# Opening of a hybrid attention and DeltaNet layer: vector products and column forms dealt among single rows of the early projections, and the token RMS factor as a diagonal in the transposing product

## The chip, the cores and the metric

The kernel runs on one core of a Trainium2 chip. The metric is the device time of one execution in microseconds (us), the median of several runs. All matrix products are in fp32, or as three products of split fp32r halves (high by high, high by low, low by high).

## The reference, cut to what matters

One layer over 512 latent tokens (x) and 256 context tokens (ctx), width 1024. The opening computes the modulated input of all projections:

```python
mod_lat = jax.nn.silu(c) @ w_mod + b_mod
mod_ctx = jax.nn.silu(c_ctx) @ w_mod + b_mod
sh1, sc1, g1, sh2, sc2, g2 = [m[:, None, :] for m in jnp.split(mod_lat, 6, axis=-1)]
csh1, csc1, cg1, csh2, csc2, cg2 = jnp.split(mod_ctx, 6, axis=-1)
hx = modulate(rms_norm(x), sh1, sc1)        # rms_norm(x) * (1 + sc1) + sh1, per token row
hc = modulate(rms_norm(ctx), csh1, csc1)
ak_x, av_x, qkv_x, db_x, da_x, aq_x, z_x, gate_x = split_cols(hx @ w_in)
```

Behind it come grouped-query attention, a bidirectional gated DeltaNet, their merge, and a gated MLP with a short convolution. The change touches none of these.

## The kernel before

All of it is one function, with a scheduler that fixes the order on each engine (TensorE = PE, VectorE = DVE, ScalarE = ACT, GpSimd = POOL, and SyncE = SP, which issues the loads) when the program is built. The opening is the block around `ORD`: a string of steps that sets the order of PE's products there; the other engines' work is placed by the scheduler around it. `k` counts the eight blocks of 128 channels, `kp` and `nb` four pairs of them. The steps:

- `dN`: `warm(N)`, 4N products of zeros into an unused PSUM buffer.
- `xj`, j = 0 to 11: `x_cols`. For tokens of tile i = j // 4 (ctx, first half of x, second half of x; each 2 x 128 tokens) and channel pair kp = j % 4, four 128x128 blocks are transposed into one PSUM buffer `pt`, which ACT or DVE copies to the stash (`hcL` for ctx, `hxL` for x). `pt` has two buffers. `j % 2 or j < XV` decides for ACT.
- `aN`, `bN`: `gemv`, the first and second half of the product of silu(c), silu(c_ctx) with columns of `w_mod` (tiles `wm`, 1 MB each) into `pm`; behind bN, ACT copies it to `mrow`.
- `mN`: `mod_cols`, which turns this row into per-channel columns `mod` and `modc` by small products into `xb` ("column form").
- `yN`: `modulate`, for channel pair N: `hf` = stash * scale + shift (DVE for x, ACT for ctx), split into a high part (`hxH`, `hcH`, on ACT) and a low part (`hxL`, `hcL`, on DVE).
- `pK`: `early_proj`, block K of the first two heads' key projections: for each head three products into `pc` (ctx, 256 wide) and three into `mb` (x, 512 wide). `qK` does the first head alone, `rK` the second.

Before the transposes each token tile is squared and summed (one half on ACT, one on DVE), POOL raises the mean to the power -1/2 into `rs`, and DVE multiplies the tile in place with it. `split(hi, lo, src)` and `load_w` produce `whi` on ACT and `wlo` on DVE from a loaded weight tile `wraw` (two buffers). The first two `wraw` are the weights of the early projections, the next three those of the next stage (`in_w_aq` twice, `in_w_av`). `LORD` sets the order of the first loads; x tiles and the `w_mod` tiles share eight buffers, so the last three of `w_mod` wait for the transposes of a token tile each. The next stage begins with the products `pq`.

Records in the profile: in the order below an fp32 product and a transpose are one row each.

Of the kernel before, what the change touches and what calls it, by code (L numbers as in the profile page):

```python
# [6 lines left out]
F32 = mybir.dt.float32  # L7
F32R = mybir.dt.float32r
AF = mybir.ActivationFunctionType
ALU = mybir.AluOpType  # L10
# [4 lines left out]
P = 128  # L15
D = 1024
KT = 8
# [17 lines left out]
POOLW = 0  # L35
ND, D0U = 4, 6
KV = 10
ORD = 'd4 x0 x1 x2 x3 x4 x5 x6 x7 a0 x8 x9 x10 x11 b0 d1 m0 y0 a1 p0 b1 p1 m1 y1 a2 b2 p2 m2 y2 p3 a3 b3 p4 m3 y3 p5 p6 p7'
RK = 1.0
HB = 2  # L40
WS = [1.0, 1.0, 1.0]
WY = [2.0, 2.4, 0.8, 0.8, 1.0, 2.4]
TG = 1
PMB = 1
XV, YV = 4, 0
NS = 2
MPA, MPD = .25, .14
DA = '203242'
# [21 lines left out]
C_ID, C_ONE, C_MS, C_MI, C_TRI = 0, 128, 256, 512, 768  # L70
# [5 lines left out]
def hybrid_layer_body(tc, x, ctxt, xT, consts, cols, rows, w_mod1, w_mod2, w_av, w_aq, w_cm, w_pa, w_pd, w_out,  # L76
                      w_up, w_down, outT, dbg=None):
    nc = tc.nc
    V, A, G, SP = nc.vector, nc.scalar, nc.gpsimd, nc.sync
    pinned = [False]  # L80

    class Ordered:
# [4 lines left out]
        def transpose(self, *a, **k):  # L87
            i = nc.tensor.transpose(*a, **k)
            return tc.keep_in_program_order(i) if pinned[0] else i
# [24 lines left out]
    def tt(out, a, b, op, eng=None):  # L114
        put((eng or V).tensor_tensor(out=out, in0=a, in1=b, op=op))  # L115

    def ts(out, a, s1, op0, s2=None, op1=None, eng=None):
        if op1 is None:
            (eng or V).tensor_scalar(out=out, in0=a, scalar1=s1, scalar2=None, op0=op0)
        else:  # L120
            (eng or V).tensor_scalar(out=out, in0=a, scalar1=s1, scalar2=s2, op0=op0, op1=op1)  # L121
# [4 lines left out]
    def act(out, a, f=AF.Copy, **kw):  # L126
        put(A.activation(out, a, f, **kw))  # L127
# [5 lines left out]
    def mm3(ps, wh, wl, xh, xl, k, n):  # L133
        T.matmul(ps, wh, xh, start=(k == 0), stop=False)
        T.matmul(ps, wh, xl, start=False, stop=False)
        T.matmul(ps, wl, xh, start=False, stop=(k == n - 1))

    def mm(ps, a, b, start=True, stop=True):
        T.matmul(ps, a, b, start=start, stop=stop)

    with es:
# [20 lines left out]
        cst = cr.tile([P, C_TRI], F32, name="cst")  # L162
        with sooner():
            SP.dma_start(cst[:, 0:C_MS], consts[:, 0:C_MS])
        ident = cst[:, C_ID:C_ID + 128]
# [19 lines left out]
        def rsqrt(out, a, s, eps):  # L185
            n = a.shape[1]
            ts(out, a, s, ALU.mult, eps, ALU.add)
            tt(out, out, mhalf[:, 0:n], ALU.pow, G)
# [8 lines left out]
        def mbank():  # L197
            return mmp.tile([P, 512], F32, name="mb", tag="mm")
# [50 lines left out]
        hxH = hxp.tile([P, KT, NL], F32R, name="hxH")  # L249
        hxL = Pairs()  # L250
# [190 lines left out]
        with m1_es:  # L441
            m1 = m1_es.enter_context(tc.tile_pool(name="m1", bufs=1))
            mps = m1_es.enter_context(tc.tile_pool(name="mps", bufs=NB, space=PSUM))
            xs = []
            wms = []

            def ordered_load(out, in_):
                i = SP.dma_start(out, in_)
                if LPIN:
                    tc.keep_in_program_order(i)  # L450

            hw = []
            for op in LORD.split():
                i = int(op[1])
# [11 lines left out]
                if op[0] == "h":  # L466
                    with first():
                        hi, lo = (m1.tile([P, 1024], F32R, name=n, tag=n, bufs=NS) for n in ("whi", "wlo"))
                        split(hi, lo, raw)
                        hw.append((hi, lo))  # L470
            with sooner():
                ordered_load(tabs.rearrange("p a b -> p (a b)"), consts[:, C_COS:C_END])
                ordered_load(wrow, rows[0:512].partition_broadcast(P))
            SP.dma_start(cst[:, C_MS:C_TRI], consts[:, C_MS:C_TRI])
            cs = m1.tile([P, 16], F32, name="cs")
            act(cs, col[:, S_C:S_C + 16], AF.Tanh, scale=0.5)
            stt(cs, cs, 1.0, col[:, S_C:S_C + 16], ALU.add, ALU.mult)
# [4 lines left out]
            V.tensor_reduce(out=sel, in_=ident.rearrange("p (b c) -> p c b", c=32)[:, 0:2, :], axis=AX.X, op=ALU.add)  # L482
            ss = m1.tile([P, 6], F32, name="ss")
            rs = m1.tile([P, 6], F32, name="rs")
            for i in range(3):
                junk = [hxH[:, k:k + 2, :].rearrange("p a b -> p (a b)") for k in (6, 2)]
                act(junk[0], xs[i][:, 0, :], AF.Square, accum_out=ss[:, 2 * i:2 * i + 1])
                V.scalar_tensor_tensor(out=junk[1], in0=xs[i][:, 1, :], scalar=1.0, in1=xs[i][:, 1, :], op0=ALU.mult, op1=ALU.mult,
                                       accum_out=ss[:, 2 * i + 1:2 * i + 2])
                sl = slice(2 * i, 2 * i + 2)  # L490
                rsqrt(rs[:, sl], ss[:, sl], 1.0 / D, EPS)
                for t in range(2):
                    ts(xs[i][:, t, :], xs[i][:, t, :], rs[:, 2 * i + t:2 * i + t + 1], ALU.mult)
            m2 = lambda t, o: t[:, o:o + 16].rearrange("p (s k) -> p s k", s=2)
            wsl = lambda k: slice(k * P, k * P + P)

# [24 lines left out]
            def x_cols(j):  # L521
                i, kp = j // 4, j % 4
                dst = stash[1][kp] if i == 0 else stash[0][kp][:, :, 256 * i - 256:256 * i]
                pt = mps.tile([P, 2, 256], F32, name="pt", tag="pt", bufs=NB - PMB - NS)
                for a in range(2):
                    for t in range(2):
                        transpose(pt[:, a, t * P:(t + 1) * P], xs[i][:, t, wsl(2 * kp + a)])
                if j % 2 or j < XV:
                    act(dst, pt)
                else:  # L530
                    V.tensor_copy(dst, pt)
# [18 lines left out]
            hps = []  # L550

            def early_proj(k, heads=slice(0, NS)):
                if not hps:
                    for _ in range(NS):
                        hps.append((mbank(), mps.tile([P, NCX], F32, name="pc", tag="pc", bufs=NS)))
                for (ps, pc), (hi, lo) in list(zip(hps, hw))[heads]:
                    mm3(pc, hi[:, wsl(k)], lo[:, wsl(k)], hcH[:, k, :], hcL[:, k, :], k, KT)
                    mm3(ps, hi[:, wsl(k)], lo[:, wsl(k)], hxH[:, k, :], hxL[:, k, :], k, KT)

            pinned[0] = True  # L560
            mrows, mpm = {}, {}
# [9 lines left out]
            def step(what, i):  # L571
                if what == "g":
                    with sooner():
                        gemv(i)
                elif what in "ab":
                    with sooner():
                        gemv(i, 0 if what == "a" else 4, 4 if what == "a" else KT)
                elif what == "m":
                    with sooner():
                        mod_cols(i, mrows[i])  # L580
                elif what == "d":
                    with sooner():
                        warm(i)
                elif what == "x":
                    with sooner():
                        x_cols(i)
                elif what == "y":
                    with first():
                        modulate(i)
                elif what in "qr":  # L590
                    early_proj(i, slice(0, 1) if what == "q" else slice(1, NS))
                else:
                    early_proj(i)

            for op in ORD.split():
                step(op[0], int(op[1:]))
# [81 lines left out]
        with kv_es:  # L678
# [31 lines left out]
            for blk in range(6):  # L710
# [5 lines left out]
                for t in range(6 if blk < 2 else 4):  # L716
# [4 lines left out]
                    for k in range(KT):  # L721
                        hi, lo = w2[k // wk]
                        wsl = slice((k % wk) * wn, (k % wk) * wn + wn)
# [692 lines left out]
        x1 = [x1p.tile([P, NL], F32, name=f"x1_{c}") for c in range(KT)]  # L1416
# [258 lines left out]
```

## Time and profile before

| | us |
|---|---|
| median of 3 runs | 1241.82 |
| lowest and highest run | 1236.42, 1242.31 |
| the profiled execution | 1239.93 |
| its span, first to last instruction | 1238.2 |
| PE busy | 1183.2 (96%) |
| DVE, ACT, POOL busy | 818.8, 601.7, 248.3 |
| first product of the stage behind the opening starts at | 56.28 |

Times in the rows are counted from the start of the span. A row of the timeline has the start, the time, the engine, the line, the operation, the tiles written and read, the shapes, the count, and in brackets the idle time ahead of it with what ended it. The granted clock is a share of TensorE's full clock.

### The profile page before, as it was taken

The page shows a single profiled execution, that of the slowest core. Times are in us where ns is not written, and L with a number is a line of the kernel's source. Part 1 is how long each engine was busy: PE and PEld are TensorE (multiplying, and loading weights), DVE is VectorE, ACT ScalarE, POOL GpSimd, SP SyncE. Part 2 cuts the span into 40 slices and gives each one's busy share as a digit, 9 for nine tenths or more (in the row PEclk, how much of TensorE's full clock was granted, in tenths as well). Part 3 has the DMA queues.
Part 4 walks back from the last instruction along what each step waited for, and adds up shares of the span by engine and source line. Part 5 has one row for each costly group of instructions (what it writes and reads, how often), then busy time and mean ns, then how long its engine had stood idle before and what let it go on. Part 6 is the DMA issues. An engine that isn't in the chain of part 4 may idle for free.

```text
span 1238.2 us, 20489 instructions
## 1 busy us (share of the span) xinstructions
PE 1183.2 (96%) x7753; PEld 1015.6 (82%) x7753; DVE 818.8 (66%) x1611; ACT 601.7 (49%) x1386; POOL 248.3 (20%) x334
## 2 busy tenths in 40 slices
PE   7999899999899898999999989999999999999996
PEld 5799888989787787788887678789888888888886
DVE  5648678888698657766657677866776765553333
ACT  4524477877565845744535432333544444432321
POOL 0111110100314695595574000000000000000000
PEclk8999999999999998999999999999999999999998
DMA  9413313332536426335336776862333422333331
GB/s 385 143 60 117 99 56 97 113 100 89 191 130 213 132 90 205 116 122 194 129 97 202 243 251 204 304 223 103 119 122 133 136 93 95 102 92 97 94 94 68
DMA packets 67554, 174.97 MB, mean 141 GB/s; under 512 B 7456, under 2 KB 18176, under 8 KB 66048
## 3 DMA queue, kind: packets, MB, share of 16 engines
q1 hardware_dynamic: 67456, 173.67, 41.8%
q8 instruction: 61, 1.00, 0.3%
q14 instruction: 37, 0.30, 0.1%
HBM read 146.85 MB, written 26.79 MB: 140 GB/s over the span
## 4 chain that ended last, share of the span: by engine, by line
PE 53%; DMA 4%; DVE 4%; ACT 2%; issue 1%; POOL 1%; SPq 0%; POOLq 0%; DVEq 0%; ACTq 0%
PE mc L84 33%; PE mb L84 13%; PE pb L84 5%; DMA gt<-atd 1%; DVE wlo L115 1%; DMA M<-gamdr 1%; PE pk L84 1%; ACT whi L127 0%; DMA wl<-in_w_mod_dram 0%; PE pqk L84 0%; DMA sz<-gdr 0%; POOL NN L115 0%; DMA cw<-in_rows_dram 0%; DMA Gb<-gamdr 0%; DMA NN<-gamdr 0%
## 5 line engine op out<-in xcount | busy, mean ns | idle before, releaser
L115 DVE TENSOR_TENSOR wlo<-wraw,whi 128x1024 fp32r<-128x1024 f32 (+1 forms) x153 | 188.7, 1235 | 159.9 <-ACT whi L127 159.5
L127 ACT ACTIVATE whi<-wraw 128x1024 fp32r<-128x1024 f32 (+1 forms) x153 | 159.5, 1044 | 213.8 <-PE mc L84 114.0
L84 PE MATMUL mc<-h,whi 128*128 128x512 f32 (+1 forms) x752 | 219.6, 376 | 0.3 <-ACT whi L127 0.3
L84 PE MATMUL mb<-hxH,whi 128*128 128x512 f32 x384 | 162.5, 423 | 1.6 <-DVE t L124 1.6
L84 PEld LDWEIGHTS mc<-h,whi 128*128 128x128 f32 x752 | 138.0, 188 | 26.1 <-ACT whi L127 0.5
L84 PE MATMUL mb<-hxL,whi 128*128 128x512 f32 x384 | 152.2, 396 | 0.2 <-DVE hxL L115 0.2
L84 PE MATMUL mb<-hxH,wlo 128*128 128x512 f32 x384 | 152.2, 396 | 0.0
L84 PE MATMUL mc<-h,wlo 128*128 128x512 f32 (+1 forms) x376 | 141.3, 376 | 0.5 <-DVE wlo L115 0.5
L84 PE MATMUL mc<-a,whi 128*128 128x512 f32 (+1 forms) x396 | 111.1, 366 | 0.6 <-DVE x L124 0.6
L115 POOL TENSOR_TENSOR rc<-rc,mhalf 128x2 f32<-128x2 f32 x4 | 3.0, 740 | 456.8 <-DVE rc L121 456.8
L84 PEld LDWEIGHTS mb<-hxH,wlo 128*128 128x128 f32 x384 | 73.0, 190 | 16.8
L84 PEld LDWEIGHTS mb<-hxH,whi 128*128 128x128 f32 x384 | 73.4, 191 | 11.9 <-issue 2.0
L84 PEld LDWEIGHTS mc<-a,whi 128*128 128x128 f32 x396 | 71.5, 189 | 12.9 <-DVE x L124 0.8
L84 PEld LDWEIGHTS mc<-h,wlo 128*128 128x128 f32 x376 | 70.8, 188 | 13.6 <-DVE wlo L115 1.0
L84 PEld LDWEIGHTS mb<-hxL,whi 128*128 128x128 f32 x384 | 73.5, 191 | 9.7 <-DVE hxL L115 0.5
L84 PE MATMUL mc<-a,wlo 128*128 128x512 f32 (+1 forms) x198 | 72.3, 365 | 0.0
L124 DVE SCALAR_TENSOR_TENSOR u<-mc,col,u 128x511 f32<-128x511 f32 x88 | 65.3, 746 | 1.4
L115 POOL TENSOR_TENSOR prod<-X,R 128x31 f32<-128x31 f32 (+15 forms) x93 | 55.5, 597 | 19.1 <-DVE X L115 12.3
L115 POOL TENSOR_TENSOR R<-R,prod 128x31 f32<-128x31 f32 (+15 forms) x93 | 56.5, 607 | 6.8
L84 PE MATMUL pq<-whi,hxH 128*128 128x256 f32 (+1 forms) x192 | 55.5, 289 | 0.0
L84 PE MATMUL pq<-wlo,hxH 128*128 128x256 f32 (+1 forms) x192 | 54.3, 283 | 0.1
L84 PE MATMUL pq<-whi,hxL 128*128 128x256 f32 (+1 forms) x192 | 54.2, 282 | 0.0
(323 smaller groups left out, 2692.1 us busy)
## 6 DMA issues: line engine op xcount, KB each, us to landing
wraw<-in_w_cm_dram SPq DMA_DIRECT2D x48, 512.0 KB, 3.6
wraw<-in_w_up_dram SPq DMA_DIRECT2D x44, 512.0 KB, 3.3
wl<-in_w_mod_dram SPq DMA_DIRECT2D x24, 512.0 KB, 4.9
wm<-in_w_mod_dram SPq DMA_DIRECT2D x8, 1024.0 KB, 16.6
wraw<-in_w_down_dram SPq DMA_DIRECT2D x16, 512.0 KB, 3.5
wraw<-in_w_aq_dram SPq DMA_DIRECT2D x10, 512.0 KB, 3.8
M<-gamdr SPq DMA_DIRECT2D x64, 64.0 KB, 4.5
wraw<-in_w_pa_dram SPq DMA_DIRECT2D x8, 512.0 KB, 4.4
```

Of the source, the lines that this page charges most:

```text
L84: i = nc.tensor.matmul(*a, **k)
L115: put((eng or V).tensor_tensor(out=out, in0=a, in1=b, op=op))
L124: V.scalar_tensor_tensor(out=out, in0=a, scalar=s, in1=b, op0=op0, op1=op1)
L127: put(A.activation(out, a, f, **kw))
```

## The change

Six things, all in the opening:

- `ORD` has seven warming steps ahead of the transposes and none behind; b0 runs ahead of the last two transposing steps; and most steps p become a q and an r, between which vector products and column forms stand.
- The token tiles are not scaled. Instead a diagonal matrix `dgx` with the RMS factors (identity times `rs`, 128x128 per 128 tokens) is the moving operand of the transposing product, which is an fp32 product now and no transpose.
- `XV` is 0: DVE copies out every even `pt` from the first on.
- Each step's products for x (`mb`) run ahead of those for ctx (`pc`), and a p does both heads' `mb` first.
- The load of the masks (`cst`, 256 KB) keeps its place behind the row vectors in SP's order.
- The scheduler, for this order, puts the splits of the next stage's weights elsewhere (below).

```diff
-ORD = 'd4 x0 x1 x2 x3 x4 x5 x6 x7 a0 x8 x9 x10 x11 b0 d1 m0 y0 a1 p0 b1 p1 m1 y1 a2 b2 p2 m2 y2 p3 a3 b3 p4 m3 y3 p5 p6 p7'
+ORD = 'd7 x0 x1 x2 x3 x4 x5 x6 x7 a0 x8 x9 b0 x10 x11 m0 y0 a1 q0 b1 r0 q1 m1 y1 r1 a2 p2 b2 q3 m2 y2 r3 a3 p4 b3 q5 m3 y3 r5 p6 p7'
-XV, YV = 4, 0
+XV, YV = 0, 0
...
-            SP.dma_start(cst[:, C_MS:C_TRI], consts[:, C_MS:C_TRI])
+                ordered_load(cst[:, C_MS:C_TRI], consts[:, C_MS:C_TRI])
...
+            dgs = []
...
                 rsqrt(rs[:, sl], ss[:, sl], 1.0 / D, EPS)
+                dgs.append(m1.tile([P, 2, P], F32, name="dgx", tag="dgx", bufs=3))
                 for t in range(2):
-                    ts(xs[i][:, t, :], xs[i][:, t, :], rs[:, 2 * i + t:2 * i + t + 1], ALU.mult)
+                    ts(dgs[i][:, t, :], ident, rs[:, 2 * i + t:2 * i + t + 1], ALU.mult)
...
-                        transpose(pt[:, a, t * P:(t + 1) * P], xs[i][:, t, wsl(2 * kp + a)])
+                        mm(pt[:, a, t * P:(t + 1) * P], xs[i][:, t, wsl(2 * kp + a)], dgs[i][:, t, :])
...
-                for (ps, pc), (hi, lo) in list(zip(hps, hw))[heads]:
+                some = list(zip(hps, hw))[heads]
+                for (ps, pc), (hi, lo) in some:
+                    mm3(ps, hi[:, wsl(k)], lo[:, wsl(k)], hxH[:, k, :], hxL[:, k, :], k, KT)
+                for (ps, pc), (hi, lo) in some:
                     mm3(pc, hi[:, wsl(k)], lo[:, wsl(k)], hcH[:, k, :], hcL[:, k, :], k, KT)
-                    mm3(ps, hi[:, wsl(k)], lo[:, wsl(k)], hxH[:, k, :], hxL[:, k, :], k, KT)
```

First place: DVE, from the squares of the ctx tile (the row that writes `ss`) to the first copies out of `pt`. Before:

```order
7 L488 SCALAR_TENSOR_TENSOR hxH,ss<-xs 128x1024
8 L121 TENSOR_SCALAR rs<-ss 128x2
9 L119 TENSOR_SCALAR xs<-xs,rs 128x1024 x2
10 L488 SCALAR_TENSOR_TENSOR hxH,ss<-xs 128x1024
11 L121 TENSOR_SCALAR rs<-ss 128x2
12 L119 TENSOR_SCALAR xs<-xs,rs 128x1024 x2
13 L488 SCALAR_TENSOR_TENSOR hxH,ss<-xs 128x1024
14 L531 COPY hxL<-pt 128x2x256
15 L121 TENSOR_SCALAR rs<-ss 128x2
```

And after the change, the same stretch of DVE:

```order
7 L489 SCALAR_TENSOR_TENSOR hxH,ss<-xs 128x1024
8 L121 TENSOR_SCALAR rs<-ss 128x2
9 L119 TENSOR_SCALAR dgx<-cst,rs 128x128 x2
10 L489 SCALAR_TENSOR_TENSOR hxH,ss<-xs 128x1024
11 L121 TENSOR_SCALAR rs<-ss 128x2
12 L119 TENSOR_SCALAR dgx<-cst,rs 128x128 x2
13 L489 SCALAR_TENSOR_TENSOR hxH,ss<-xs 128x1024
14 L533 COPY hcL<-pt 128x512
15 L121 TENSOR_SCALAR rs<-ss 128x2
```

Row 14 was the copy of step x4 (to `hxL`), since ACT copied x0 to x3; now it is the copy of x0 (to `hcL`), behind the squares of all three token tiles.

Second place: DVE around the third `modulate`, y2. Before, from the column form m2 on:

```order
34 L115 TENSOR_TENSOR mod<-xb,col 128x2x2
35 L115 TENSOR_TENSOR modc<-xb,col 128x2x2
36 L121 TENSOR_SCALAR hf<-hxL,mod 128x512 x2
37 L115 TENSOR_TENSOR hxL<-hf,hxH 128x512
38 L115 TENSOR_TENSOR hcL<-hf,hcH 128x256
39 L115 TENSOR_TENSOR hxL<-hf,hxH 128x512
40 L115 TENSOR_TENSOR hcL<-hf,hcH 128x256
41 L115 TENSOR_TENSOR wlo<-wraw,whi 128x1024
42 L115 TENSOR_TENSOR mod<-xb,col 128x2x2
```

After, DVE again, from m2 to m3:

```order
37 L115 TENSOR_TENSOR mod<-xb,col 128x2x2
38 L115 TENSOR_TENSOR modc<-xb,col 128x2x2
39 L121 TENSOR_SCALAR hf<-hxL,mod 128x512 x2
40 L115 TENSOR_TENSOR wlo<-wraw,whi 128x1024
41 L115 TENSOR_TENSOR hxL<-hf,hxH 128x512 x2
42 L115 TENSOR_TENSOR wlo<-wraw,whi 128x1024
43 L115 TENSOR_TENSOR hcL<-hf,hcH 128x256 x2
44 L115 TENSOR_TENSOR wlo<-wraw,whi 128x864
45 L115 TENSOR_TENSOR mod<-xb,col 128x2x2
```

The low parts of the three weight tiles of the next stage stood behind y2 (the first), between m3 and y3 (the second) and behind y3 (the third); now all three stand inside y2. ACT's high parts `whi` moved with them, and the third (the tile of `in_w_av`) now stands ahead of `mrow` of the last vector product:

```order
24 L127 ACTIVATE whi<-wraw 128x1024
25 L127 ACTIVATE hf<-hcL,modc 128x256 x2
26 L127 ACTIVATE hxH<-hf 128x512 x2
27 L127 ACTIVATE whi<-wraw 128x1024
28 L127 ACTIVATE hcH<-hf 128x256 x2
29 L127 ACTIVATE whi<-wraw 128x864
30 L127 ACTIVATE mrow<-pm 128x512
```

These are ACT's rows after the change; before, two of these `whi` stood behind that `mrow`, and the third behind the last `hxH` of the opening.

## The prediction

> **What bounds the kernel now.** I read the page first (busy times), then the clock and the busy time by stretch, then the instructions of the first 57 us in order of time, engine by engine.
>
> ```profile
> span 1238.2 us, 20489 instructions
> PE 1183.2 (96%) x7753; PEld 1015.6 (82%) x7753; DVE 818.8 (66%) x1611; ACT 601.7 (49%) x1386; POOL 248.3 (20%) x334
> 56.28:1238.20 1181.92, 1135.58 (x7494) 983.11 (x7492) 787.52 (x1546) 573.27 (x1335) 244.48 (x322) 0.99 0.41 134
> ```
>
> The third line is a stretch: length, busy time of PE, PEld, DVE, ACT and POOL (with instruction counts), granted clock, DMA share, GB/s. TensorE carries the program. Behind 56.28 us it is busy 1135.6 of 1181.9 us at a clock of 0.99, and PE's order there is the same in both kernels. So the change is worth what it moves the first product of the next stage, which starts here:
>
> ```profile
> 56.28 0.28 PE L84 MATMUL pq<-whi,hcH 128*128 128x256 f32 x1
> 23.65 1.05 PE L84 MATMUL xb<-sel,mrow 128*128 128x2 f32 x8
> 54.17 0.28 PE L84 MATMUL pc<-hcH,whi 128*128 128x256 f32 x1
> 43.88 1.92 PE L84 MATMUL pm<-wm,cs 128*32 128x512 f32 x16
> 45.74 0.39 PE L84 MATMUL pc<-hcH,whi 128*128 128x256 f32 x1
> ```
>
> The last three give prices: a step p (one k, two heads) is 56.28 - 54.17 = 2.11 us, so a single head's q or r is 1.06; a vector product in two halves (a and b) is 45.74 - 43.88 = 1.86, so a half is 0.93. The second line is m0, the first column form: I cut the opening there, into 23.65 us before it and 32.63 us behind it.
>
> Now the clock. The following stretches have the same columns:
>
> ```profile
> 7.81:11.22 3.41, 1.08 (x8) 0.89 (x8) 2.49 (x6) 1.33 (x4) 0.70 (x1) 1.00 1.01 428
> 11.22:14.64 3.42, 3.06 (x15) 2.25 (x12) 2.50 (x6) 2.71 (x6) 0.70 (x1) 0.51 1.03 434
> 14.64:18.05 3.41, 3.40 (x18) 2.35 (x20) 2.26 (x6) 1.00 (x3) 0.70 (x1) 0.50 0.99 406
> 18.05:21.46 3.41, 3.06 (x25) 1.77 (x20) 2.02 (x4) 1.86 (x3) 0.00 (x0) 0.99 1.02 423
> 24.88:28.29 3.41, 1.70 (x12) 0.69 (x5) 2.64 (x8) 2.75 (x6) 0.00 (x0) 1.00 1.03 418
> 28.29:31.71 3.42, 3.42 (x14) 2.19 (x16) 0.39 (x2) 0.00 (x0) 0.00 (x0) 0.51 1.01 417
> ```
>
> A stretch of 3.41 us in which PE is busy for 1.08 or 1.70 us is followed by one or two at half clock. The DMA runs at 406 to 434 GB/s, full, in all of them.
>
> **The first part, to m0.** The diagonals replace six scalings of 1024 columns by six of 128, and the transposes become products.
>
> ```profile
> 1.49 5.33 PE L84 MATMUL pt<-hxH 128*128 128x512 f32 x16 [1.49 <-DVE hxH L563]
> 8.99 1.42 DVE L119 TENSOR_SCALAR xs<-xs,rs 128x1024 f32<-128x1024 f32 x2 [0.82 <-POOL rs L115]
> 10.33 1.22 DVE L488 SCALAR_TENSOR_TENSOR hxH<-xs 128x1024 fp32r<-128x1024 f32 x1
> 12.64 1.42 DVE L119 TENSOR_SCALAR xs<-xs,rs 128x1024 f32<-128x1024 f32 x2 [0.82 <-POOL rs L115]
> 13.97 1.22 DVE L488 SCALAR_TENSOR_TENSOR hxH<-xs 128x1024 fp32r<-128x1024 f32 x1
> 15.12 0.69 DVE L531 COPY hxL<-pt 128x512 f32<-128x512 f32 x1
> 1230.09 0.48 DVE L119 TENSOR_SCALAR dg<-cst,rc 128x128 f32<-128x128 f32 x2 [0.88 <-POOL rc L115]
> 9.80 0.33 PE L88 MATMUL pt<-cst,xs 128*128 128x128 f32 x1 [2.98 <-DVE xs L119]
> 11.70 6.24 PE L88 MATMUL pt<-cst,xs 128*128 128x128 f32 x24 [0.22 <-ACT hcL L127]
> 11.05 1.09 ACT L127 ACTIVATE hcL<-pt 128x512 f32<-128x512 f32 x2 [0.69 <-PE pt L88]
> 20.43 1.09 PE L88 MATMUL pt<-cst,xs 128*128 128x128 f32 x8 [0.35 <-DVE hxL L531]
> L84 PE MATMUL mc<-dg,cst 128*128 128x128 f32 x16 | 3.0, 319 | 1.5 <-DVE dg L119 1.5
> L119 DVE TENSOR_SCALAR dg<-cst,rc x8: 278/284/288, 856.3 to 1230.3; 128x128 f32<-128x128 f32 x8
> 449.86 1.06 PE L84 MATMUL pb<-S,kT 128*128 128x128 f32 x8
> ```
>
> DVE: two diagonals cost 0.48 us (the dg row, the same operation at the program's end) in place of 1.42, so 0.94 is saved per token tile, 2.8 in all, on an engine with room. PE: each dg tile is used by one product, and eight of them left 16 records, so an fp32 product is two passes. A transpose left one (48 transposes in this kernel, 48 records). Eight passes of 128 columns take 1.06 us (the row at 449.86), of which some 0.17 is the drain of the last: 0.89 back to back. So an x step (four products) costs 0.89 at full clock; two steps of transposes took 1.09 at 20.43, about 0.5 each. That is 12 x 0.4 = 4.7 us more for PE. The twelve added warming products fill the idle 2.98 us ahead of 9.80 (16 took 5.33, the later ones at 0.235, so 28 end at about 9.5): free, since x0 is held by the first diagonal until 9.8 anyhow.
>
> Step x2 is where the time goes. It needs the PSUM buffer of x0 (two buffers), which ScalarE emptied at 11.05, so x2 ran at 11.70. Now VectorE empties x0 (XV = 0), and on its queue that copy stands behind the squares of x1 and x2. From the rows: first diagonals at 8.99, squares of x1 at 8.99 + 0.40 = 9.39; from squares to the next scaling 12.64 - 10.33 = 2.31, so second diagonals at 11.70, squares of x2 at 12.10; to the copy 15.12 - 13.97 = 1.15, so it starts at 13.25 and ends 0.69 later. x2 starts at 14.0 and not 11.7.
>
> From there PE has ten x steps (8.9), a0 and b0 (1.9) to m0; with two buffers a pair of steps takes 0.89 and 0.17 of drain, 0.69 of copy and 0.14 of signals, 1.89 or 0.945 a step, 0.5 more. That is 14.0 + 8.9 + 1.9 + 0.5 = 25.3 at full clock. But PE idles from about 11.5 to 14.0, more than the 2.3 us that it idled in the stretch 7.81 to 11.22, which cost it the clock. If the clock is half for one stretch of 3.4 us, 1.7 us of work are lost, of which 0.4 are waits on copies anyhow: 26.6. I take this: **m0 is 3.0 us later** (bounds: +1.7 at full clock, +4.7 with two stretches, as before had from 11.22).
>
> [...] In 11.22:14.64 PE was busy 3.06 of 3.42 us with transposes, and the clock stayed at half for another stretch. [...]
>
> **The second part, m0 to the end.** Products are the same in number: 16 x 1.06, six halves of 0.93, four column forms. Only the waits differ. They come from what modulate needs after a column form:
>
> ```profile
> 26.06 0.62 ACT L127 ACTIVATE hxH<-hf 128x512 fp32r<-128x512 f32 x1
> 26.71 0.69 DVE L115 TENSOR_TENSOR hxL<-hf,hxH 128x512 fp32r<-128x512 f32 x1 [0.77 <-ACT hxH L127]
> 27.32 0.42 DVE L115 TENSOR_TENSOR hcL<-hf,hcH 128x256 fp32r<-128x256 f32 x1
> 24.63 1.06 PE L84 MATMUL pm<-wm,cs 128*32 128x512 f32 x8
> 27.04 0.38 PE L84 MATMUL pc<-hcH,whi 128*128 128x256 f32 x1 [1.34 <-ACT hcH L127]
> L84 PE MATMUL pc<-hcH,whi 128*128 128x256 f32 x16 | 5.2, 324 | 1.8 <-ACT hcH L127 1.8
> L84 PE MATMUL pc<-hcL,whi 128*128 128x256 f32 x16 | 4.9, 308 | 1.1 <-DVE hcL L115 1.1
> L84 PE MATMUL mb<-hxL,whi 128*128 128x512 f32 x16 | 6.9, 431 | 0.2 <-DVE hxL L115 0.2
> 49.09 1.22 DVE L115 TENSOR_TENSOR wlo<-wraw,whi 128x1024 fp32r<-128x1024 f32 x1
> wraw<-in_w_av_dram SPq DMA_DIRECT2D x2, 432.0 KB, 3.5
> ```
>
> Before, the rows of the early projections list 1.8 + 1.1 + 0.2 = 3.1 us of idle PE in six waits; each also hides a drain of some 0.16 that counts as busy, so 4.05 in all. What will they be after? The column form ended at 24.63; hxH was there 2.1 us later, hxL 2.8, the first hcL 3.1. So after each m the first row waits 2.1 us less what PE has in between, and its second product another 0.45 (0.69 less 0.235).
> - y0: cover is a1, 0.93: waits 1.2 + 0.45 = 1.65.
> - y1: cover r1 and a2, 1.99: 0.1 + 0.45 = 0.55.
> - y2: cover r3 and a3, but the splits of two weight tiles (wlo, 1.22 each) now stand on VectorE between hf and hxL and between hxL and hcL. hxL comes at 3.15, hcL at 5.2: p4 takes 3.7 and not 2.1, with the 0.1 a wait of 1.7. Before, p3, a3 and b3 covered all of y2.
> - y3: cover r5 alone, 1.06: 1.05 + 0.45 = 1.5. Before, all of p5 (2.11) was cover.
>
> After 5.4, before 4.05: **1.35 us more**. The half clock at 28.29:31.71 cost 1.7; the stretch around y0 keeps its gap of 1.2 us in my sum, so I leave that cost where it is (bounds: 1.7 less, or 1.7 more with a second one).
>
> The mask load that moves behind the row vectors lets the last three loads of w_mod land up to 0.6 us earlier (256 of 1024 KB, which take 2.5). Nothing waits for that: the last of them was issued at 19.1 and landed 16.9 us later, and b3 runs behind 43.88:
>
> ```profile
> L448 SPq DMA_DIRECT2D wm<-in_w_mod_dram x1: 328/328/328, 19.1 to 19.1; - x1
> DMA to landing us min/median/max: 16.9/16.9/16.9
> ```
>
> On SP's queue the masks now stand ahead of two weight loads, but behind the same bytes in all, so those land when they did; if the masks were late themselves, nothing of the opening would see it. The cost is nothing. The four warming products d1 (0.9 us) go, too; they lay in PE's wait for mrow0, which x10 and x11 now fill, since b0 runs ahead of them.
>
> **Sum:** 3.0 + 1.35 = 4.35 us, so the opening ends at about 60.6 and the profiled execution of 1239.93 us (span 1238.2) becomes 1244.3. I take **1244**. That execution lies 1.9 us under the median 1241.82 of the three runs, which spread from 1236.42 to 1242.31; so about 0.5% (6.2 us) is what a measurement of this kernel can tell from no change.
>
> **Rivals.**
> 1. *The clock stays up.* The x steps are real products, the warming reaches to x0, and the dealt rows leave no stretch as empty as 24.88:28.29. Then m0 comes at 25.3 (+1.65), the waits cost 1.35, and the 1.7 of 28.29:31.71 goes: +1.3, 1241.2. With y2's splits hidden as well, -0.4: 1239.5. For it: the stretch 14.64:18.05, which ended at full clock. Against it: the gap of 2.5 us ahead of x2. 0.33.
> 2. *Slower beyond 0.5%: a load in ScalarE's way.* The split of the third weight tile now stands on ScalarE ahead of mrow3 and all of y3. Its load can be issued only when the first wlo has freed a buffer, 2.5 us after m2. With the 3.5 us of the row above it lands 6.4 after m2, b3 ends at 6.6, and the 0.7 that mrow3 then waits lies under q5. From a landing of some 4.9 us on PE waits, and at 6.8 the sum passes 6.2: the time is 1246.5 at that point and 1249 at 9.5 us. For it: landings of 16.9 us while the DMA was full. Against it: it is not full behind 40 us. 0.12.
> 3. *Faster beyond 0.5%.* Would need the opening to end before 50.1. PE's work from m0 on is 25.8 us, and m0 can't come before 24.8, so 50.6 is its floor without any wait. 0.05, mostly for the spread of the runs.
>
> The forecast, +2 to +6, has 0.50. Slower by over 0.5% gets 0.15 (the second rival and the forecast's upper end), faster 0.05, within 0.80. The range goes from 1237.5 (the first rival at its best, with 2 us of spread) to 1249.
>
> **What would show it.** Right: VectorE's first copy out of pt starts at about 13.3 and x2 at 14.0; x steps at 0.9 us with 96 records of pt<-dgx,xs; m0 between 25 and 27; p4 stalled for its hcL; the first pq at 60 to 61. Wrong: a clock of 1.0 through 11 to 32 us (rival 1), ScalarE waiting for the DMA of in_w_av ahead of mrow (rival 2), or a first pq before 56.

## The result: 3.8 us slower, in the size forecast

The changed kernel takes 1243.14 us (median of 20 runs), the kernel before 1239.36 (median of 20, the three shown above among them). The ratio is 1.0030, with a 95% interval of 1.0018 to 1.0043. One of the changed kernel's 20 runs took 1965.29 us at a granted clock of 0.555 and is left out of the ratio; without it the median is 1242.92. The prediction was 1244.0, from a sum of 4.35 us. The two profiled executions differ by 4.04 us: 1243.97 against 1239.93.

The page of the profile after, span and busy times:

```profile
span 1242.2 us, 20603 instructions
PE 1191.4 (96%) x7809; PEld 1025.7 (83%) x7809; DVE 817.5 (66%) x1613; ACT 600.6 (48%) x1384; POOL 247.0 (20%) x334
```

The stretch behind the opening (columns as before: length; busy time of PE, PEld, DVE, ACT, POOL; granted clock, DMA share, GB/s):

```profile
59.70:1242.20 1182.50, 1138.11 (x7495) 986.31 (x7493) 788.17 (x1548) 573.24 (x1336) 244.06 (x322) 0.99 0.41 134
```

Behind the first `pq` lie 1182.50 us, before 1181.92. So the loss is in the opening, whose end moved from 56.28 to 59.70 (3.42 us). PE's instructions there in order of time, of the changed kernel:

```profile
10.30 1.95 PE L84 MATMUL pt<-dgx,xs 128*128 128x128 f32 x16
13.22 2.05 PE L84 MATMUL pt<-dgx,xs 128*128 128x128 f32 x16 [0.97 <-ACT hcL L127]
15.81 3.99 PE L84 MATMUL pt<-dgx,xs 128*128 128x128 f32 x32 [0.54 <-DVE hcL L533]
19.73 1.06 PE L84 MATMUL pm<-wm,cs 128*32 128x512 f32 x8
...
25.59 0.95 PE L84 MATMUL xb<-sel,mrow 128*128 128x2 f32 x8
...
28.52 0.50 PE L84 MATMUL mb<-hxH,whi 128*128 128x512 f32 x1 [0.97 <-ACT hxH L127]
...
44.41 0.51 PE L84 MATMUL mb<-hxH,whi 128*128 128x512 f32 x1
45.36 0.50 PE L84 MATMUL mb<-hxL,whi 128*128 128x512 f32 x1 [0.44 <-DVE hxL L115]
47.43 0.39 PE L84 MATMUL pc<-hcL,whi 128*128 128x256 f32 x1 [0.53 <-DVE hcL L115]
48.22 1.06 PE L84 MATMUL pm<-wm,cs 128*32 128x512 f32 x8
53.35 0.49 PE L84 MATMUL mb<-hxH,whi 128*128 128x512 f32 x1 [0.87 <-ACT hxH L127]
57.53 0.46 PE L84 MATMUL mb<-hxH,whi 128*128 128x512 f32 x1
59.70 0.28 PE L84 MATMUL pq<-whi,hcH 128*128 128x256 f32 x1
```

m0, the first column form, starts at 25.59, 1.94 later than before; from m0 to `pq` it is 34.11 us, 1.48 more. DVE and ACT at the two places that the prediction speaks of, step x2 and y2:

```profile
12.59 0.58 ACT L127 ACTIVATE hcL<-pt 128x512 f32<-128x512 f32 x1
13.10 0.69 DVE L533 COPY hcL<-pt 128x512 f32<-128x512 f32 x1
44.62 1.28 DVE L115 TENSOR_TENSOR hxL<-hf,hxH 128x512 fp32r<-128x512 f32 x2
45.83 1.22 DVE L115 TENSOR_TENSOR wlo<-wraw,whi 128x1024 fp32r<-128x1024 f32 x1
46.96 0.75 DVE L115 TENSOR_TENSOR hcL<-hf,hcH 128x256 fp32r<-128x256 f32 x2
48.09 0.92 ACT L127 ACTIVATE whi<-wraw 128x864 fp32r<-128x864 f32 x1 [1.70 <-DMA wraw<-in_w_av_dram]
49.36 0.60 ACT L127 ACTIVATE mrow<-pm 128x512 f32<-128x512 f32 x1 [0.34 <-PE pm L84]
```

And the stretches of the changed kernel; the clock is the third number from the end:

```profile
11.22:14.64 3.42, 2.45 (x22) 2.26 (x21) 2.30 (x6) 1.63 (x3) 1.00 (x2) 1.00 1.02 431
14.64:18.05 3.41, 2.87 (x24) 2.60 (x23) 1.77 (x4) 0.75 (x2) 0.00 (x0) 1.00 1.00 408
24.88:28.29 3.41, 2.66 (x24) 1.74 (x23) 1.89 (x5) 2.04 (x4) 0.00 (x0) 1.00 1.00 418
28.29:31.71 3.42, 2.97 (x16) 1.55 (x17) 1.97 (x4) 1.63 (x5) 0.00 (x0) 1.00 1.02 426
52.18:55.60 3.42, 2.32 (x8) 1.52 (x7) 2.35 (x5) 2.25 (x6) 0.00 (x0) 0.80 0.04 14
55.60:59.02 3.42, 3.42 (x15) 2.96 (x15) 0.00 (x0) 0.53 (x1) 0.00 (x0) 0.70 0.00 0
```

The clock is full where before it was half (0.51, 0.50 and 0.51 in 11.22 to 18.05 and 28.29 to 31.71). Instead, p6 behind the wait for y3 runs at half clock: it takes 57.53 - 53.35 = 4.18 us, where 2.11 and the small wait in it make 2.5.

### The profile page after: what moved, and what is told of

Same layout as the page of the kernel before. It is cut to its first block, busy times and chain, and to the rows that moved or that the text cites. A ratio compares the mean times of both kernels' runs of the same rounds, so it can differ in the third digit from the quotient of the medians.

```text
span 1242.2 us, 20603 instructions
## 1 busy us (share of the span) xinstructions
PE 1191.4 (96%) x7809; PEld 1025.7 (83%) x7809; DVE 817.5 (66%) x1613; ACT 600.6 (48%) x1384; POOL 247.0 (20%) x334
## 4 chain that ended last, share of the span: by engine, by line
PE 54%; DVE 4%; DMA 3%; ACT 2%; issue 1%; SPq 0%; POOLq 0%; DVEq 0%; ACTq 0%
PE mc L84 33%; PE mb L84 14%; PE pb L84 6%; DMA gt<-atd 1%; DVE wlo L115 1%; PE pk L84 1%; DMA sz<-gdr 0%; DMA wl<-in_w_mod_dram 0%; ACT whi L127 0%; PE pqk L84 0%; DMA M<-gamdr 0%; DVE wl L394 0%; DMA tdr<-go 0%; DVE o_nt L1017 0%; ACT NN L127 0%
## 5 line engine op out<-in xcount | busy, mean ns | idle before, releaser
L124 DVE SCALAR_TENSOR_TENSOR t<-mb,col,t 128x511 f32<-128x511 f32 (+1 forms) x76 | 48.9, 644 | 10.7 <-ACT t L127 10.5
```

The lines of the kernel that those rows point to most:

```text
L124: V.scalar_tensor_tensor(out=out, in0=a, scalar=s, in1=b, op0=op0, op1=op1)
```

## The experiments

All ratios are to the kernel before, with a 95% interval. "The opening's end" is the start of the first `pq` in the one profiled execution of each. Of e5, e6 and e8 the numbers stand in the text alone. The moved load of the masks, the fifth item of the change, was not run by itself.

### e1: the dealt order alone

The kernel before, with the new `ORD` and nothing else of the change.

```diff
-ORD = 'd4 x0 ... x9 x10 x11 b0 d1 m0 y0 a1 p0 b1 p1 m1 y1 a2 b2 p2 m2 y2 p3 a3 b3 p4 m3 y3 p5 p6 p7'
+ORD = 'd7 x0 ... x9 b0 x10 x11 m0 y0 a1 q0 b1 r0 q1 m1 y1 r1 a2 p2 b2 q3 m2 y2 r3 a3 p4 b3 q5 m3 y3 r5 p6 p7'
```

> The kernel before with the changed ORD alone (seven warming steps, b0 ahead of x10, dealt q and r); transposes, scaled token tiles, XV = 4 and the old order of mb and pc stay. My theory (the products in fp32 make m0 late, the dealt order costs some 1.5 us behind m0): m0 comes at about 21.5 us, since the transposes run at full clock behind the warming and x8 is held by the scaling of the last token tile; behind m0 34 us as in the changed kernel; first pq at 55.5 to 56, so 0 to 1 us faster than before. Rival (the dealt order is what costs, whatever the transposes do): first pq at 58 or later, 2 us or more slower. Rival (the dealt order gains, and the products eat it): first pq at 53 to 54, 2 to 3 us faster.

Measured: 1245.35 us, ratio 1.0052 (1.0032 to 1.0071). PE's rows in order of time, and then two stretches of this kernel:

```profile
21.55 1.05 PE L84 MATMUL xb<-sel,mrow 128*128 128x2 f32 x8
26.22 0.58 PE L84 MATMUL pc<-hcH,whi 128*128 128x256 f32 x1 [2.62 <-ACT hcH L127]
61.57 0.28 PE L84 MATMUL pq<-whi,hcH 128*128 128x256 f32 x1
```

```profile
24.88:28.29 3.41, 1.90 (x5) 1.51 (x6) 2.21 (x5) 2.11 (x5) 0.00 (x0) 0.53 1.01 416
28.29:31.71 3.42, 3.42 (x14) 1.10 (x14) 0.00 (x0) 0.60 (x1) 0.00 (x0) 0.50 1.02 424
```

m0 came 2.1 us earlier than before, and the opening ended 5.3 later. With little work left between m0 and y0's first row PE waits 2.62 us there and then runs two stretches at half clock; y2 (1.13 and 0.99) and y3 (1.17 and 0.37) wait as well. In this kernel, too, the scheduler puts a `wlo` (at 45.28) ahead of y2's low parts, so e1 prices the order together with where it puts the splits. The order is a loss by itself, by the runs (1.0052) as large as the whole change or larger: what m0 gained was more than lost behind it.

### e2: the diagonals alone, and e3: the change with XV = 4

```diff
e2, against before:
+                dgs.append(m1.tile([P, 2, P], F32, name="dgx", tag="dgx", bufs=3))
-                    ts(xs[i][:, t, :], xs[i][:, t, :], rs[...], ALU.mult)
+                    ts(dgs[i][:, t, :], ident, rs[...], ALU.mult)
-                        transpose(pt[...], xs[i][:, t, wsl(2 * kp + a)])
+                        mm(pt[...], xs[i][:, t, wsl(2 * kp + a)], dgs[i][:, t, :])
e3, against the changed kernel:
-XV, YV = 0, 0
+XV, YV = 4, 0
```

> The kernel before with the diagonals alone (fp32 products in place of transposes, no scaling of the token tiles); ORD, XV = 4 and the order of mb and pc stay. My theory: twelve x steps of 0.98 us at full clock, of which those ahead of 14.6 us run at half clock since the warming ends at 6.8; m0 at 26 us, 2.4 later than before, and nothing regained behind it: 2.5 us slower (first pq at 58 to 59). Rival (the products keep the clock up and so pay for themselves): no stretch at half clock behind 14.6 us, the one around 28 to 32 us gone, m0 at 25 and first pq at 56: no difference.

> The changed kernel with XV = 4 again (ScalarE copies x0 to x3). My theory of the late x2: without the copy behind the squares on VectorE x2 starts about 1 us earlier, and the 0.5 us gap ahead of x4 goes; m0 at 24.2 instead of 25.6, the rest the same: 1.0 to 1.5 us faster than the changed kernel, some 2.5 us slower than before. Rival (PE's 96 passes set the stage, the copies are hidden): m0 stays at 25.5 and the time at 3.8 us slower than before.

Measured: e2 1240.58 us, ratio 1.0018 (1.0002 to 1.0034), m0 at 24.49, the opening's end at 59.77. e3 1242.39 us, ratio 1.0029 (1.0009 to 1.0050), m0 at 25.08, only 0.5 us ahead of the changed kernel's: less than the 1.0 to 1.5 us expected. First PE and ACT of e2, then ACT and PE of e3, around the third step x:

```profile
9.40 4.85 PE L84 MATMUL pt<-dgx,xs 128*128 128x128 f32 x40 [1.40 <-DVE dgx L119]
10.59 0.60 ACT L127 ACTIVATE hcL<-pt 128x512 f32<-128x512 f32 x1 [0.16 <-PE pt L84]
12.93 1.05 ACT L127 ACTIVATE hxH<-xs 128x1024 fp32r<-128x1024 f32 x1
```

```profile
11.76 1.06 ACT L127 ACTIVATE hxH<-xs 128x1024 fp32r<-128x1024 f32 x1 [1.31 <-DMA xs<-in_x_dram]
12.81 1.07 ACT L127 ACTIVATE hcL<-pt 128x512 f32<-128x512 f32 x2
13.45 3.79 PE L84 MATMUL pt<-dgx,xs 128*128 128x128 f32 x31 [1.83 <-ACT hcL L127]
```

In e3 ACT copies x0 and x1 again, and x2 still starts at 13.45: the copies stand on ACT behind its squares of the third token tile (11.76). In e2, ACT copies x0 at 10.59 ahead of those squares (12.93), and PE runs x0 to x4 without a gap. So the wait at x2 does not come from VectorE's turn in the copies. The changed kernel, e3 and e10 (below), all with d7, have it (0.97, 1.83, 0.98 us) and e2, with d4, does not. That the longer warming alone moves ACT's order is seen in e6 (below), the kernel before with d7 and nothing else: there the squares of the third tile (12.17) stand behind one copy (11.51), where before they stood (13.34) behind three (11.05 for two of them, 12.85). By what rule the scheduler does this was not tried.

Two things are to be read from e2. Its clock was 1.00 from 4.4 to 24.9 us and its x2 did not wait, and m0 came 0.84 us later than before (1.03 later than in e6, which also has the full clock there): this is about what the products cost by themselves. Behind m0 it lost 2.65 us more than before, for reasons that are not the products': two stretches at half clock, from 27.5 to 34.4, where before had one, and a wait at y3. ACT and PE of e2:

```profile
51.42 0.93 ACT L127 ACTIVATE whi<-wraw 128x864 fp32r<-128x864 f32 x1 [2.32 <-DMA wraw<-in_w_av_dram]
54.73 0.39 PE L84 MATMUL pc<-hcH,whi 128*128 128x256 f32 x1 [1.75 <-ACT hcH L127]
```

ACT waited 2.32 us for the load of `in_w_av`, with all of y3 behind it on its queue, and then PE waited 1.75 us for y3. This is the mechanism of the prediction's second rival, in another kernel.

### e4 and e5: the splits and the tail

e4 is the changed kernel with PE's order unchanged, but the splits of the first two next weight tiles behind y2 and the third behind y3. e5 is the changed kernel with the old end of `ORD`.

```diff
e4:
-... m2 y2 r3 a3 p4 b3 q5 m3 y3 r5 p6 p7
+... m2 y2 r3 a3 p4 w0 b3 q5 m3 y3 w1 r5 p6 p7     (w0, w1: load_w of the next stage here; modulate's splits of y2 and y3 are kept in program order)
e5:
-... r3 a3 p4 b3 q5 m3 y3 r5 p6 p7
+... r3 a3 b3 p4 m3 y3 p5 p6 p7
```

> The changed kernel, PE's order untouched, with the splits of the next stage's weights taken out of y2: the first two (whi on ScalarE, wlo on VectorE) stand behind y2, the third behind y3. My theory (the low parts of y2 come late because of these splits): p4, which took 3.8 us from its first product to b3, takes 2.6; first pq 1.2 us earlier than in the changed kernel, about 2.5 us slower than before. Rival (the wait is only put off, to y3 or to the clock): p4 is shorter but the first pq stays within 0.4 us of 59.7.

> The changed kernel with the old tail of the order (a3 b3 p4 m3 y3 p5 p6 p7 in place of a3 p4 b3 q5 m3 y3 r5 p6 p7); the rest stays dealt. My theory (the dealt order leaves only r5, 1.06 us, as cover of y3, and the gap takes p6 to half clock): the wait of 0.9 us ahead of p6 goes, p6 runs at full clock (1.6 us), and p4 starts 0.9 later behind the same low parts (0.7): first pq at 56.5 to 57, 3 us earlier than in the changed kernel, within 1 us of before. If the clock has nothing to do with it: 1.6 us earlier. Rival (what costs is the dealing at y0 and y1 and the late m0): 0.5 us earlier at most.

Measured: e4 1242.25 us, ratio 1.0013 (1.0000 to 1.0027), the opening's end at 57.38. PE's p4 in e4, up to b3:

```profile
45.41 0.50 PE L84 MATMUL mb<-hxL,whi 128*128 128x512 f32 x1 [0.17 <-DVE hxL L115]
47.46 1.07 PE L84 MATMUL pm<-wm,cs 128*32 128x512 f32 x8
```

p4 begins at 44.74 and takes 2.72 us, against 48.22 - 44.41 = 3.81: the two `wlo` inside y2 cost 1.1. In e4 p6 also ran at full clock, with the same wait ahead of it (0.87 and 0.23): 2.7 us in place of 4.18. With m0 0.33 later this makes 2.2 of the 2.3 us by which the opening ended earlier. So the half clock at p6 is not settled by the order. By the runs e4 lies between both kernels, its interval overlaps that of the changed kernel, and the gain is not shown in the whole time. e5: 1243.44 us, ratio 1.0027 (1.0009 to 1.0044), the opening's end at 57.99, although in that execution m0 came only at 27.01, after a stretch at clock 0.53 in 14.64 to 18.05; from m0 on it took 30.98 us, 3.1 less than the changed kernel, of which 1.7 is the half clock at p6 that this execution did not have. The old tail alone makes no difference that the runs can tell.

### e6, e7, e8, e11: more warming

```diff
e6, against before:
-'d4 x0 ...
+'d7 x0 ...
e7 (and e11, the same kernel again), against before:
-'d4 x0 ... m0 y0 a1 p0 ...
+'d7 x0 ... m0 y0 a1 d2 p0 ...
e8, against the changed kernel:
-... y3 r5 p6 p7'
+... y3 r5 d1 p6 p7'
```

> The kernel before with d7 in place of d4 alone. [...] Rival (the half clock in 11 to 18 us is what makes the opening late): a0 at 15 to 16, m0 at 21.5, 2 us faster.

> The kernel before with d7 in place of d4 and eight more warming products (d2) behind a1, in PE's gap ahead of p0. My theory of the clock: the stretch that ran at half clock from 28.3 us on runs at full clock, 1.7 us less, of which up to 0.4 is lost since eight products take 1.9 us where the gap is 1.5: first pq at 54.5, 1.5 us faster than before. Rival (that stretch is slow for another reason, the loads): first pq at 56 to 56.5.

> The changed kernel with four warming products (0.94 us) in PE's gap between r5 and p6. My theory of the clock: p6 runs at full clock and takes 2.6 us instead of 4.2, first pq 1.5 us earlier than in the changed kernel (58.2), 2.3 us slower than before. Rival (p6 is slow for another reason): first pq stays at 59.7.

> The kernel before with d7 and d2 once more, unchanged, to see whether its 0.9967 comes again. Theory: the clock stays at 1.00 through 24.88 to 31.71 us, the first pq comes at about 54.2, and the ratio is 0.996 to 0.998. Rival: the gain was the luck of where the half-clock stretches behind the opening fell (its profiled execution had only two of them), and the ratio is 0.999 to 1.001.

| | median us | ratio (95%) | m0 | opening's end |
|---|---|---|---|---|
| e6 | 1237.41 | 0.9991 (0.9973 to 1.0008) | 23.46 | 55.88 |
| e7 | 1236.03 | 0.9967 (0.9952 to 0.9982) | 23.09 | 54.19 |
| e11 | 1236.00 | 0.9968 (0.9951 to 0.9985) | 23.07 | 54.15 |
| e8 | 1243.67 | 1.0024 (1.0009 to 1.0039) | 25.76 | 58.26 |

Two stretches of e11, and its first `pq`:

```profile
24.88:28.29 3.41, 3.41 (x19) 2.57 (x16) 2.44 (x6) 2.35 (x6) 0.00 (x0) 1.00 1.01 406
28.29:31.71 3.42, 3.42 (x23) 2.04 (x22) 0.00 (x0) 0.60 (x1) 0.00 (x0) 1.00 1.01 424
```

```profile
54.15 0.28 PE L84 MATMUL pq<-whi,hcH 128*128 128x256 f32 x1
```

Eight products of zeros between a1 and p0 fill y0's wait, the clock stays full where before it was 0.51, and the opening ends 2.1 us earlier, 0.3 more than the first of the two texts had. The kernel with d7 and d2 is faster than both kernels in question, by 0.3% against before, in two sets of runs. These 0.3% are 4.0 us in the medians; the opening's 2.1 explain half of it, and where the rest lies the single profiles do not tell. d7 alone (e6) filled the half clock at 11 to 18 and won 0.2 us at m0: that half clock had been hidden behind the loads and copies. The clock was 1.00 in both stretches there (11.22:14.64 and 14.64:18.05 of e6) with 2.13 and 2.60 us of work on PE, transposes but for the start of a0, so in this run they held it. In e8 the profile did as expected (p6 at full clock), the median did not follow.

### e9 and e10: mb first, and the products, each at full clock

e9 is e7 with the change's order of rows in a step (both heads' `mb`, then both `pc`). e10 is e9 with the diagonals and products.

```diff
e9, against e7:
-                for (ps, pc), (hi, lo) in list(zip(hps, hw))[heads]:
-                    mm3(pc, ...)
-                    mm3(ps, ...)
+                some = list(zip(hps, hw))[heads]
+                for (ps, pc), (hi, lo) in some:
+                    mm3(ps, ...)
+                for (ps, pc), (hi, lo) in some:
+                    mm3(pc, ...)
e10, against e9: the lines of e2
```

> The kernel before with the warming d7 in place of d4 and d2 behind a1, and the changed kernel's order inside a step of the early projections (both heads' mb rows ahead of both pc rows), with transposes and the old order of steps. Theory: a second head's mb products cover the second product's wait for the low part hcL, so y1's waits of about 0.85 us in all shrink to 0.2 and y3's likewise; first pq at about 53.3, 1 us ahead of the kernel with d7 and d2 alone, and the median 4 to 5 us under the kernel before. Rival: the rows' order only moves the wait to another row; first pq at about 54.2 and the same ratio as with d7 and d2 alone, 0.997.

> The kernel with d7, d2 and the dealt rows of a step, and in it the diagonals with products in place of the transposes; the order of steps and XV = 4 stay as before. The clock should be full on both sides, so this prices the products alone. Theory: an x step costs 0.98 in place of about 0.5 us, and what of it the load of the token tiles doesn't hide is 1 to 2 us at m0; first pq 1 to 2 us later than in the kernel without diagonals, and the median 1 to 2 us above it. Rival: the products pay for themselves (VectorE's shorter scalings bring x0 and x2 forward and the rest is hidden): no difference within 0.5 us at m0 and in the median.

Measured: e9 1238.84 us, ratio 0.9981 (0.9966 to 0.9997); e10 1242.03 us, ratio 1.0012 (0.9994 to 1.0029). m0, y3's wait and the first `pq` of e9, then x2, m0 and the first `pq` of e10:

```profile
23.45 1.05 PE L84 MATMUL xb<-sel,mrow 128*128 128x2 f32 x8
49.50 0.50 PE L84 MATMUL mb<-hxL,whi 128*128 128x512 f32 x1 [0.49 <-DVE hxL L115]
53.57 0.28 PE L84 MATMUL pq<-whi,hcH 128*128 128x256 f32 x1
```

```profile
13.72 5.84 PE L84 MATMUL pt<-dgx,xs 128*128 128x128 f32 x48 [0.98 <-ACT hcL L127]
26.44 0.95 PE L84 MATMUL xb<-sel,mrow 128*128 128x2 f32 x8
56.17 0.28 PE L84 MATMUL pq<-whi,hcH 128*128 128x256 f32 x1
```

The clock is 1.00 from 4.4 to 62 us in both, so this is the price of the edit without the clock: m0 3.0 us later, the opening's end 2.6, the median 3.2 (the two intervals overlap by a little). The theory that it costs was right, its size (1 to 2 us) too small. But it is not the price of the products alone. In e10 x0 starts only behind the warming, at 10.79, and x2 waits for ACT's copies behind the squares; e2, at full clock as well, starts x0 at 9.40, has no such wait, and reaches m0 at 24.49, 1.04 later than e9. So some 1 us of the 3.0 is the products', by comparison of two profiles, and the other 2 go with the late start of x2. With transposes a late start costs little: x0 of e9 starts at 10.61, that of e11 at 9.87, and their m0 are 0.4 apart. Of e9 the profile bore out half (opening 0.6 us shorter than e7's, y1's wait 0.41, y3's 0.49), and the runs the contrary: its median is 2.8 us above that of e11, which ran beside it. The intervals overlap (0.9966 to 0.9997 and 0.9951 to 0.9985), and where the 2.8 us would be, the single profiles do not tell. This stays open.

## Why the prediction was right, point by point

The opening's end in three profiled executions at a time gives the account: before 56.28; with full clock and the new rows in a step (e9) 53.57, which is 2.71 less; with the products and their late x2 (e10) 56.17, 2.60 more; with the dealt order and its splits, XV = 0 and without d1 and d2 (the changed kernel) 59.70, 3.53 more, of which 1.7 is the half clock at p6. The change brings two losses, which e1 and e2 show singly in the runs, and keeps the clock at the two places where before lost it, which by itself would have been a gain (e11).

Two of the three signs that the text gave for being wrong did appear: the clock was 1.00 from 11 to 32 us, and ScalarE waited for the load of `in_w_av` ahead of `mrow`. That the time still came out within 1 us of 1244 is in part luck: the cost of the dealt order and of the late x2 was rightly foreseen, but several terms of the sum were off, and they cancelled.

- **The first part: 3.0 us forecast, 1.94 measured.** At full clock the text had 25.3; m0 came at 25.59. Inside it the sizes were off and cancelled. x2 started at 13.22 and not at 14.0. Behind it 1.07 us more went by than the text had. An x step back to back is 0.89 us, as forecast: x0 and x1, right behind the warming, took 1.95 for 16 passes, where eight take 1.06 (the row at 449.86 of before): 0.89 for eight more, and 0.17 at the end of a row, which the text calls drain. What the sum lacked is a price for each start: a pair of steps behind a wait or a vector product took 2.05 (13.22, 20.73), and the four from 15.81 to 19.73, with one stop inside and the turn to a0 at the end, 3.92 where 4 x 0.89 is 3.57; some 0.75 in all. The wait ahead of x4 was 0.70 with its drain (0.54 listed), where the text had 0.5 for all copies (the 0.14 of signals in it no row shows; x4 began 0.05 behind the copy that released it, 15.07 + 0.69 to 15.81, and the copy of x3 0.04 behind its product, 13.22 + 2.05 to 15.31), and a half took 1.00 (19.73 to 20.73) and not 0.93.
- **The warming was not free at x0.** The text had the 28 products end at about 9.5 and x0 held until 9.8 by the first diagonal. They ended at 10.30, and x0 started then, though the first diagonals were done at 9.33. In this execution it cost nothing, since x2 waited for ScalarE in any case; but the warming also moved ScalarE's order (e6).
- **The step that was wrong: what holds x2.** The text had it wait for VectorE's copy of x0. That copy started at 13.10 (13.25 forecast) and took 0.69, but x2 began at 13.22, while it was still running: x2 was released by ScalarE's copy of x1 (12.59), so it was not x0's buffer that it needed, and e3 shows that x2 waits as long without VectorE's turn. The queue that counted was ScalarE's, with the squares of the third token tile ahead of the copies. The forecast got nearly the right time (14.0 for 13.22) from the wrong queue, which is luck.
- **The half clock behind x2: 1.3 us taken, none came.** PE's gap there was 0.97 us and not 2.5 us, since d7 and x0, x1 reached to 12.25. The stretch 11.22:14.64 had PE busy for 2.45 us and the clock stayed at 1.00. Here the first rival was right.
- **The second part: 1.35 forecast, 1.48 measured, with other terms.** The waits listed are 0.97 + 0.23 (y0), 0.17 (y1), 0.44 + 0.53 (y2) and 0.87 + 0.23 (y3), 3.44 in all; with 0.16 of drain for each of the seven (a `pc` row is listed with 0.28 us and the next begins 0.12 behind it, as at 29.82, 29.93 and 30.05), 4.56 against 4.05 before: 0.5 more and not 1.35. p4's wait was 3.81 - 2.11 = 1.70, as forecast. The other 1.0 us is in the pieces: a vector product by halves is 2.00 and not 1.86, and a single head's row, where one was timed between two other steps without a wait, took 1.15 (q3) or 1.23 (r1) and not 1.06. This term was missing.
- **One half clock in place of another.** The text kept the 1.7 us of 28.29:31.71 at y0; it went from there and came back at p6. The sum stood, the place was not the one named. In e4 and e8 p6 ran at full clock, and their medians are within 1 us of the changed kernel's, so the result does not hang on it.
- **The second rival, the load of `in_w_av` ahead of mrow3**, came and cost nothing here: ACT waited 1.70 us for it, split the tile from 48.09 on, and then still stood idle for 0.34 us until the product that `mrow` needs was done; the text had mrow3 wait 0.7. In e2 the same wait cost PE 1.75 us, so its place on the queue is a real risk. In the rival's sum 1239.93 + 4.35 + 1.9 makes 1246.2 and not 1246.5; nothing hangs on that.
- **Transposes and the clock.** The first rival counts on the x steps being products. That this matters for the clock was not shown: in e11's stretch 11.22:14.64 PE ran nothing but transposes, 2.16 us of busy time, and the clock stayed at 1.00 there and behind it. Before, at half clock, 3.06 us of them in 11.22:14.64 were followed by another stretch at 0.50 (the rows that the text shows).

## What to carry to other kernels

Where two steps of an order are cut into halves so as to fill waits, count first what filled those waits already: here the dealt order brought the first column form forward by 2.1 us and lost 7.4 behind it (e1). The clock that fell to 0.51 behind a stretch in which PE stood idle for 1.71 us (24.88:28.29 of before) was mended here by eight products of zeros in the gap (d7 and d2 together gained 0.3% of the whole time; d7 alone, e6, nothing that its interval can tell), and not by moving real work into it. And before a wait is put down to one engine's copy, look at what stands ahead of the copies on every engine that could make them: here it was the other one's squares. And a price taken from one kernel holds for the order of that kernel: the same products cost some 1 us at m0 in e2 and 3.0 in e10, where the copies stood behind the squares.

## What the runs showed of the hardware

The half-clock stretches lie on a grid of 3.41 us whose phase differs from execution to execution. In the clock records of the two traces every piece at half clock but the last is 3.413 or 6.827 us long in before, 3.413 in the changed kernel, and the pieces at full clock between them are whole multiples of 3.413 (in both 37.547, 51.200 and 501.759 us are among them, 11, 15 and 147 times). Where the clock changes, in stretches of 0.40 us of before, the changed kernel and e2:

```profile
28.20:28.60 0.40, 0.40 (x3) 0.36 (x3) 0.40 (x2) 0.00 (x0) 0.00 (x0) 0.69 0.92 389
```

```profile
54.00:54.40 0.40, 0.33 (x1) 0.33 (x2) 0.40 (x3) 0.40 (x2) 0.00 (x0) 0.81 0.00 0
```

```profile
27.20:27.60 0.40, 0.00 (x0) 0.00 (x0) 0.15 (x1) 0.40 (x2) 0.00 (x0) 0.93 1.03 435
```

A mean of 0.69 between 1.0 and 0.5 puts the change at 28.35 (0.25 us ahead of the end), 0.81 at 54.25, 0.93 at 27.54. Less whole multiples of 3.413 these are 1.05, 3.05 and 0.24. So the same gap falls into one stretch in one execution and is cut in two in another. The same place of the program, in before and in the changed kernel, each by its own grid:

```profile
513.04:516.45 3.41, 2.58 (x20) 1.77 (x15) 3.41 (x5) 3.37 (x11) 3.35 (x4) 1.00 0.47 153
516.45:519.87 3.42, 2.64 (x12) 2.17 (x12) 1.25 (x2) 3.35 (x8) 3.11 (x6) 1.00 0.20 53
```

```profile
518.47:521.88 3.41, 1.34 (x6) 0.86 (x5) 2.31 (x3) 3.34 (x11) 3.35 (x5) 1.00 0.34 131
521.88:525.29 3.41, 3.41 (x9) 2.53 (x9) 2.56 (x3) 2.14 (x3) 3.02 (x6) 0.50 0.59 177
```

Before, the gap is shared by two stretches with 2.6 us of work each, and the clock stays; in the changed kernel it lies in one, with 1.34 us of work, and the next runs at half, 1.7 us lost. Cut so, the five profiles of before, the changed kernel, e1, e2 and e5 have 29 full-clock stretches in which PE was busy for 0.52 to 1.62 us, and 28 of them are followed by half clock; of 47 with 1.66 to 2.34 us five are (1.71, 1.95, 1.96 and twice 2.31), all in the opening; of the 1634 with more none. What decides between 1.66 and 2.34 was not shown.

For the reading of results this matters: the time behind the first `pq`, where PE's work is the same, was 1174.6 us in e7's profiled execution and 1184.0 in e8's, and the 34 runs of before that stood beside e7 spread from 1233.09 to 1243.79. Up to 1220 us e7's profile has two stretches at half clock behind its opening and e8's has seven; five at 1.7 us each would be 8.5 of the 9.4 us between them, by estimate. So a single profile can lie several us off its kernel's median, and differences of one or two us are seen only in medians of many runs, or in the opening's own rows.
